# Seven products for eight in a quarter of the contraction: two output projections and one gate of a decoder trunk

## The chip, the cores and the metric

The kernel runs on one core of a Trainium2 chip. The metric is device time in microseconds of one execution of the whole program. TensorE (PE) multiplies, VectorE (DVE) and ScalarE (ACT) do the work on elements, GpSimd (POOL) and SyncE (SP) mostly issue DMAs. Each engine takes its instructions in the order in which they were built.

## What is computed

The reference is a decoder trunk of two layers on 256 tokens of 2048 features, in float32. Each layer has a norm, a wide input projection, a token mixer (two recurrences in layer 0, a matrix memory in layer 1), an output projection added to the residual `h`, and a gated embedding. The lines that matter here, for both layers `i`:

```python
h = x
for i in range(DEPTH):
    ...
    mix = y @ e_w_out[j]            # layer 0; layer 1: yc @ o_w_out[j]
    h = h + mix
    pl = rmsnorm(p[i] @ ple_w[i], ple_norm[i])
    h = h + jax.nn.sigmoid(h @ ple_gate_w[i]) * pl
return rmsnorm(h, final_norm)
```

All the products of `h` or `y` with a 2048 x 2048 matrix are alike: 256 tokens, 2048 inputs, 2048 outputs.

## The kernel before

**A product.** Each float32 operand is split into a high and a low part, and three matmuls (high by high, high by low, low by high) stand for one. The activations are stationary: `act[j]` (tiles `ahl`) holds 256 input features of all 256 tokens, high and low. The weights move. A product with a 2048 x 2048 matrix goes in four chunks of 512 outputs; a chunk has two token halves of 128, each with its own PSUM bank, and takes the 2048 inputs in four quarters (`quarter_tok`, line 185). A quarter of one token half is 4 x 3 = 12 matmuls of 512 columns, so a chunk is 96. A quarter's weights come as two pieces of 128x1024 (512 KB each), read by SP into a ring of five tiles (`raw`). ACT casts each piece to its high part (`whi`, line 135) and DVE subtracts that to get the low part (`wlo`, line 136), in rings of four.

**Order of the work.** The program is written as generators. `project_two` (line 171) interleaves the quarters of chunks 0 and 1, so that a product can begin when only the first input features are there; `chunks` (line 180) appends the chunks 2 and 3. Side work (hops, splits of new activations, norms) is put into lanes and taken a step at a time by `pump` after each first token half. A scheduler then orders each engine's instructions by priority: loads' splits stand 400 ahead of their place in the text, other work at its place. `tc.issue_after(ins)` ties what is traced under it behind `ins` on the same engine.

**Seven for eight.** The first layer-1 gates (`oog`, `oz`) already use a scheme in which two chunks of outputs, two token halves and two halves of a quarter (or of two quarters) form a 2 x 2 by 2 x 2 block product: seven products of combinations of blocks stand for eight products of blocks. `combos` (line 231) makes four combinations of the activations (numbers 1 to 4, tiles `q4`) and splits them; `seven` (line 262) loads four weight pieces X, Y, W, Z of the quarter, adds them into each other on DVE, splits each state, and issues seven products of six matmuls into four PSUM banks A, F, E, B. The quarters that are left out of the scheme go through `plain` (line 222). After the first product (A) ACT copies A's bank to F and, negated, to B; E begins with the product of combination 4 and the state of Y. Halves are combined from PSUM and from SBUF tiles named `pr`.

**After a chunk.** In an output projection (`out_proj`, line 553) DVE adds both banks to the residual tile `hq[c]`. In the gate (`ple_gate`, line 565) ACT takes a tanh and two fused DVE operations scale it and add it to `hq[c]`. Then `to_features` (line 519) turns the chunk into the next product's activations: DVE transposes blocks (tile `w`, line 523), POOL writes them to DRAM and reads them back in four gathers (`across`, line 639 and 642), and ACT and DVE split them. The gathers wait in POOL's queue for the write to land.

**The residual tiles** `hq` are four tiles of 128 x 1024. In layer 0 POOL reads them from the input `x` (`load_hq`, line 1064): two before the output projection, the other two from within `mixed` (line 1070), at the chunks 1 and 2, each tied behind the last hop issued. In layer 1 POOL reads all four from DRAM copies (`home`, line 1382) before the output projection.

## Time and profile before

| | us |
|---|---|
| time, median of 3 runs | 1027.11 (1026.71 to 1027.2) |
| time of the profiled execution | 1026.88 |
| its span, first to last instruction | 1025.1 |
| TensorE busy | 1015.3 |
| DVE busy | 787.6 |
| ACT busy | 632.2 |
| POOL busy | 105.2 |

The profile is of one execution. Times of rows count from the first instruction. Matmuls overlap, so that a row's own length (0.39) is longer than the step from one to the next. L and a number is a line of the kernel before; a tile is named without its number.

### The profile page before, as it was taken

The numbers are of one execution on the slowest core, as the hardware profiler recorded it, in microseconds if no ns is written. First come the engines' busy times: TensorE is split into PE (matmuls) and PEld (weight loads), VectorE is DVE, ScalarE is ACT, GpSimd is POOL, SyncE is SP. The second block draws the span as 40 slices with busy tenths as digits, with TensorE's granted clock in tenths as the row PEclk, the third lists the DMA queues.
The fourth block names the chain that finished last, engine by engine and source line by source line (L and its number), as shares of the span: only waits on it lengthen the run. The fifth ranks groups of instructions, "written<-read, shape, count | busy, mean of one in ns | idle before, by whom it ended". The sixth has DMA issues, their size and how long they took to land. (4 is left out here: it accounts for less than half of the span.)

```text
span 1025.1 us, 14447 instructions
## 1 busy us (share of the span) xinstructions
PE 1015.3 (99%) x5188; PEld 843.8 (82%) x5188; DVE 787.6 (77%) x1163; ACT 632.2 (62%) x909; POOL 105.2 (10%) x190
## 2 busy tenths in 40 slices
PE   9999999999999999999999999999999999999996
PEld 8888888888888888888888888888888888888886
DVE  7858968969685775776559997878889996766684
ACT  7775554686974344565457876766676777344562
POOL 0111101011112121021011100000011112111000
PEclk9999999999999999999999999999999999999999
DMA  9988756568788898698798755357879889788652
GB/s 356 340 223 252 221 177 199 170 201 240 221 262 285 271 283 256 222 307 255 224 297 246 231 184 190 124 188 200 257 193 285 222 279 337 248 254 260 222 185 82
DMA packets 69672, 242.14 MB, mean 236 GB/s; under 512 B 9024, under 2 KB 10432, under 8 KB 69600
## 3 DMA queue, kind: packets, MB, share of 16 engines
q1 hardware_dynamic: 54720, 193.36, 57.4%
q0 software_dynamic: 14448, 47.33, 17.2%
q8 instruction: 40, 0.66, 0.3%
q10 hardware_dynamic: 432, 0.52, 0.1%
q14 instruction: 32, 0.26, 0.1%
HBM read 221.26 MB, written 19.92 MB: 235 GB/s over the span
## 5 line engine op out<-in xcount | busy, mean ns | idle before, releaser
L136 DVE TENSOR_TENSOR wlo<-raw,whi 128x1024 fp32r<-128x1024 f32 (+1 forms) x329 | 396.8, 1215 | 164.7 <-ACT whi L135 155.4
L135 ACT CAST whi<-raw 128x1024 fp32r<-128x1024 f32 (+1 forms) x329 | 343.6, 1048 | 258.2 <-PE mm L198 184.0
L196 PE MATMUL mm<-whi,ahl 128*128 128x512 f32 x960 | 375.1, 391 | 0.0
L197 PE MATMUL mm<-wlo,ahl 128*128 128x512 f32 x960 | 373.7, 389 | 0.0
L198 PE MATMUL mm<-whi,ahl 128*128 128x512 f32 x960 | 373.6, 389 | 0.0
L196 PEld LDWEIGHTS mm<-whi,ahl 128*128 128x128 f32 x960 | 180.2, 188 | 38.0 <-issue 0.8
L198 PEld LDWEIGHTS mm<-whi,ahl 128*128 128x128 f32 x960 | 180.2, 188 | 37.5
L197 PEld LDWEIGHTS mm<-wlo,ahl 128*128 128x128 f32 x960 | 180.3, 188 | 37.0
L217 PE MATMUL mm<-whi,ahl 128*128 128x512 f32 x244 | 77.9, 390 | 0.8 <-ACT mm L314 0.8
L196 PE MATMUL mx<-whi,ahl 128*128 128x512 f32 x160 | 62.2, 389 | 0.0
L197 PE MATMUL mx<-wlo,ahl 128*128 128x512 f32 x160 | 62.2, 389 | 0.0
L198 PE MATMUL mx<-whi,ahl 128*128 128x512 f32 x160 | 62.2, 389 | 0.0
L207 DVE TENSOR_TENSOR wlo<-ch,whi 128x1024 fp32r<-128x1024 f32 x41 | 49.5, 1222 | 8.2 <-ACT whi L206 6.9
L217 PEld LDWEIGHTS mm<-whi,ahl 128*128 128x128 f32 x244 | 45.8, 188 | 10.6 <-ACT mm L314 1.3
L217 PE MATMUL mm<-wlo,ahl 128*128 128x512 f32 x122 | 47.5, 390 | 0.0
L206 ACT CAST whi<-ch 128x1024 fp32r<-128x1024 f32 x41 | 42.8, 1053 | 7.6 <-PE mm L217 5.4
L217 PE MATMUL mx<-whi,ahl 128*128 128x512 f32 x128 | 41.6, 389 | 0.0
L217 PE MATMUL mm<-whi,q 128*128 128x512 f32 x112 | 37.1, 389 | 0.0
L197 PEld LDWEIGHTS mx<-wlo,ahl 128*128 128x128 f32 x160 | 30.0, 188 | 6.3
L196 PEld LDWEIGHTS mx<-whi,ahl 128*128 128x128 f32 x160 | 30.0, 188 | 6.2
L198 PEld LDWEIGHTS mx<-whi,ahl 128*128 128x128 f32 x160 | 30.0, 188 | 6.2
L217 PEld LDWEIGHTS mx<-whi,ahl 128*128 128x128 f32 x128 | 24.0, 188 | 5.0
(372 smaller groups left out, 1129.1 us busy)
## 6 DMA issues: line engine op xcount, KB each, us to landing
raw<-in_ew_dram SPq DMA_DIRECT2D x64, 512.0 KB, 5.0
raw<-in_g_dram SPq DMA_DIRECT2D x64, 512.0 KB, 4.6
raw<-in_eo_dram SPq DMA_DIRECT2D x32, 512.0 KB, 5.6
raw<-in_oqk_dram SPq DMA_DIRECT2D x32, 512.0 KB, 4.4
raw<-in_ov_dram SPq DMA_DIRECT2D x32, 512.0 KB, 4.2
raw<-in_oo_dram SPq DMA_DIRECT2D x32, 512.0 KB, 5.3
raw<-in_oog_dram SPq DMA_DIRECT2D x24, 512.0 KB, 4.1
raw<-in_oz_dram SPq DMA_DIRECT2D x20, 512.0 KB, 5.2
```

The source lines that it names most:

```text
L135: last["act"] = s.copy(h, r).ins
L136: last["dve"] = v.tensor_tensor(out=l, in0=r, in1=h.bitcast(F32), op=ALU.subtract).ins
L196: te.matmul(ps[hf], xh, wh, start=(k == 0), stop=False)
L197: te.matmul(ps[hf], xh, wl, start=False, stop=False)
L198: last["pe"] = te.matmul(ps[hf], xl, wh, start=False, stop=(k == KT - 1)).ins
L206: last["act"] = s.copy(hi, r).ins
L207: last["dve"] = v.tensor_tensor(out=lo, in0=r, in1=hi.bitcast(F32), op=ALU.subtract).ins
L217: last["pe"] = te.matmul(o, x, y, start=(first and k + i == 0), stop=(end and k == n - 1 and i == 2), skip_group_check=True).ins
```

## The change

It does four things.

1. A new generator `two_and_seven` takes the place of `chunks` in both output projections and in the first gate (`g0`). Chunks 0 and 1 stay as they are; chunks 2 and 3 go through `seven`, with the scheme on the first quarter of the contraction (512 inputs) and the three other quarters plain. The combinations are started when chunk 0 has been handed on, and drained when chunk 1 has.
2. In the two output projections `seven` is given `home`, the first token half of `hq[3]`: ACT copies it into bank E after the copies of A, E's product accumulates onto it, and the last sum goes straight into `hq[3]`, so that the add for that half falls away. Without `home` (the gate, and the older uses) E begins with its product. In layer 0, `hq[2]` and `hq[3]` are now read at chunk 0 and chunk 1.
3. In `product`, the first matmul is tied behind the last matmul traced before it, so that the products of a section stand on TensorE in the order of the text.
4. `combos` works on a whole pair of token halves at once: combinations 3 and 1 in one tile and one split, then 2 and 4 in another.

The core of the diff:

```diff
+    def two_and_seven(w, act, before, places, home=None):
+        qs = {}
+        for c, ps in enumerate(project_two(w, act, before)):
+            for hf in range(2):
+                yield c, hf, ps[hf]
+            if c == 0:
+                room, part, *where = places()
+                start("combos", combos(act, 0, qs, *where))
+        drain("combos")
+        for b, hf, src in seven(w, 2, act, qs, (0,), room, part, home and home()):
+            yield 2 + b, hf, src
...
-                last["pe"] = te.matmul(o, x, y, start=(first and k + i == 0), stop=(end and k == n - 1 and i == 2),
-                                       skip_group_check=True).ins
+                with ExitStack() as behind:
+                    if k + i == 0:
+                        behind.enter_context(tc.issue_after(last["pe"]))
+                    last["pe"] = te.matmul(o, x, y, start=(first and k + i == 0), stop=(end and k == n - 1 and i == 2),
+                                           skip_group_check=True).ins
...
+        a11, a21 = whole(0)
+        a12, a22 = whole(1)
+        c, (c3, c1) = pair()
+        less(c3, a21, a11)
+        less(c1, a21, a22)
+        keep(c, (3, 1))
         yield
+        d, (c2, c4) = pair()
+        less(c2, a11, c1)
+        less(c4, a12, c2)
+        keep(d, (2, 4))
         yield
...
         with tc.high_priority(offset=450):
             s.copy(F, A)
             s.activation(B, A, AF.Copy, scale=-1.0)
+            if home is not None:
+                s.copy(E, home)
         Y = load(room, 1, 1)
-        product(E, combo(4), split(Y), True)
+        product(E, combo(4), split(Y), home is None)
...
-        soon(g, E, g, ALU.add)
-        yield 1, 0, g
+        if home is None:
+            soon(g, E, g, ALU.add)
+            yield 1, 0, g
+        else:
+            soon(home, E, g, ALU.add)
+            yield 1, 0, None
...
-        for c, ps in enumerate(chunks(a["eo"], 4, y, ready(y, "fm"))):
-            if c in (1, 2):
-                load_hq(c + 1, last["hop"])
+        for c, hf, src in two_and_seven(a["eo"], y, ready(y, "fm"), in_e0, lambda: hq[3][:, 0]):
+            if hf == 0 and c < 2:
+                load_hq(c + 2, last["hop"])
...
-    acth = ple_gate(hq, a["g0"], act, pls, rp0, hss0, "on", "fg", ready(act, "fe"), gate_sums)
+    acth = ple_gate(hq, two_and_seven(a["g0"], act, ready(act, "fe"), in_e0), pls, rp0, hss0, "on", "fg", gate_sums)
...
-        act = out_proj(hq, chunks(a["oo"], 4, y, ready(y, "fm")), "fo")
+        act = out_proj(hq, two_and_seven(a["oo"], y, ready(y, "fm"), in_m1, lambda: hq[3][:, 0]), "fo")
```

How instructions stand now, in layer 0's output projection. TensorE first, before: the end of chunk 1 (bank `mx_3064`) and the beginning of chunk 2 (bank `mm_3407`).

```order
L196 MATMUL mx_3064<-whi_3364,ahl_3286 128x512
L197 MATMUL mx_3064<-wlo_3365,ahl_3286 128x512
L198 MATMUL mx_3064<-whi_3364,ahl_3286 128x512
L196 MATMUL mm_3407<-whi_3410,ahl_2785 128x512 [waits Activation_49]
L197 MATMUL mm_3407<-wlo_3411,ahl_2785 128x512 [waits DVE_49]
L198 MATMUL mm_3407<-whi_3410,ahl_2785 128x512
L196 MATMUL mm_3407<-whi_3410,ahl_2785 128x512
```

And now: `mx_3426` is bank A, `mm_3428` is bank E, `q4_3423` holds combinations 2 and 4, `whi_3447` and `wlo_3448` are the split of Y.

```order
L211 MATMUL mx_3064<-whi_3367,ahl_3286 128x512
L233 MATMUL mx_3426<-whi_3432,ahl_2785 128x512 [waits Activation_49]
L233 MATMUL mx_3426<-wlo_3433,ahl_2785 128x512 [waits DVE_49]
L233 MATMUL mx_3426<-whi_3432,ahl_2785 128x512 x2
L233 MATMUL mx_3426<-wlo_3433,ahl_2785 128x512
L233 MATMUL mx_3426<-whi_3432,ahl_2785 128x512
L233 MATMUL mm_3428<-whi_3447,q4_3423 128x512 [waits DMAHW3_49,DMAHW2_49,DMAHW6_49,DVE_49,Activation_49]
L233 MATMUL mm_3428<-wlo_3448,q4_3423 128x512 [waits DVE_49]
L233 MATMUL mm_3428<-whi_3447,q4_3423 128x512 [waits DVE_49]
L233 MATMUL mm_3428<-whi_3447,q4_3423 128x512
L233 MATMUL mm_3428<-wlo_3448,q4_3423 128x512
```

Chunk 2 began with a quarter that needs only activations and weights; now it begins with A, and E, which needs a combination, stands directly behind A.

DVE at the same place, before: from the first add of chunk 1 (`hq_3059<-mx_3063`) on.

```order
L560 TENSOR_TENSOR hq_3059<-mx_3063,hq_3059 128x512
L515 TENSOR_TENSOR pl_153<-pl_153,row_3341 128x512
L136 TENSOR_TENSOR wlo_3448<-raw_3446,whi_3447 128x1024
L560 TENSOR_TENSOR hq_3059<-mx_3064,hq_3059 128x512
L136 TENSOR_TENSOR wlo_3454<-raw_3452,whi_3453 128x1024
L523 STREAM_TRANSPOSE w_3397<-hq_3059 128x4x4x32 x2
L515 TENSOR_TENSOR pl_157<-pl_157,row_3341 128x512
```

And now: `ch_3430`, `ch_3445`, `raw_3457` are X, Y, W; `wlo_3463` and `wlo_3469` belong to the plain quarter behind E, `wlo_3499` to the product behind that; `w_3349` is the transpose of chunk 0, `w_3410` that of chunk 1, and `q4_3423` the low part of combinations 2 and 4.

```order
L549 STREAM_TRANSPOSE w_3349<-hq_3057 128x4x4x32
L304 TENSOR_TENSOR raw_3457<-raw_3457,ch_3430 128x1024
L136 TENSOR_TENSOR wlo_3463<-raw_3461,whi_3462 128x1024
L136 TENSOR_TENSOR wlo_3469<-raw_3467,whi_3468 128x1024
L304 TENSOR_TENSOR ch_3430<-ch_3430,ch_3445 128x1024
L220 TENSOR_TENSOR wlo_3499<-raw_3457,whi_3498 128x1024
L586 TENSOR_TENSOR hq_3059<-mx_3064,hq_3059 128x512
L264 TENSOR_TENSOR q4_3391<-qc_3388,q4_3391 128x512
L549 STREAM_TRANSPOSE w_3410<-hq_3059 128x4x4x32 x2
L255 TENSOR_TENSOR qc_3420<-xr_3384,qc_3388 128x256
L541 TENSOR_TENSOR pl_153<-pl_153,row_3343 128x512
L255 TENSOR_TENSOR qc_3420<-xr_3386,qc_3420 128x256
```

The low part `q4_3423` is the row behind these. The sums of the weights and three splits that TensorE uses after E now stand between chunk 0's transpose and the combinations that E uses. In the first gate and in layer 1's output projection the same six weight operations stand ahead of combinations 2 and 4.

POOL's queue, before: `hq_3393` is `hq[2]`, `hq_3557` is `hq[3]`.

```order
L639 DMA dfe0_3351<-w_3347 128x1024
L642 DMA r_3350<-dfe0_3351 32x4x256 x4
L1064 DMA hq_3393<-in_x_dram 128x2x512
L639 DMA dfe1_3401<-w_3397 128x1024
L642 DMA r_3400<-dfe1_3401 32x4x256 x4
L1064 DMA hq_3557<-in_x_dram 128x2x512
L639 DMA dfe2_3565<-w_3561 128x1024
```

And now: `hq_3337` is `hq[2]`, `hq_3406` is `hq[3]`.

```order
L1092 DMA hq_3337<-in_x_dram 128x2x512
L533 DMA row_3343<-in_rows_dram 128x1024
L533 DMA row_3345<-in_rows_dram 128x1024
L1124 MEMSET wg_3789 128x512
L667 DMA dfe0_3353<-w_3349 128x1024
L670 DMA r_3352<-dfe0_3353 32x4x256 x4
L1092 DMA hq_3406<-in_x_dram 128x2x512
L667 DMA dfe1_3414<-w_3410 128x1024
```

`hq[2]` moved ahead of the first hop, and `hq[3]` from behind the second hop to behind the first.

## The prediction

> **What bounds the kernel now.** I read the page first, then the waits of TensorE, the stretches around the three places that change, and the timelines of VectorE (DVE), GpSimd (POOL) and ScalarE (ACT) there.

> ```profile
> span 1025.1 us, 14447 instructions
> PE 1015.3 (99%) x5188; PEld 843.8 (82%) x5188; DVE 787.6 (77%) x1163; ACT 632.2 (62%) x909; POOL 105.2 (10%) x190
> PE mm L217 <- ACT mm L314: 0.8, 1, 0.8
> PE st L97 <- PEq L1634: 0.8, 1, 0.8
> 686.95 21.76 PE mm L217 x96
> ```

> TensorE works through 1015.3 of 1025.1 us, and its table of waits holds only 1.6 us. So the time is the number of matmuls times their rate, and the rate stands in the last row (the chain of waits): 96 matmuls of 512 columns begin within 21.76 us, 0.2267 us each. Anything else costs time only if it makes TensorE wait; a wait of TensorE, on the other hand, costs its full length, since there is no slack to take it up.

> The second halves (chunks 2 and 3) of the three products, in the table by stretches (columns: PE, PEld, DVE, ACT, POOL busy, clock, DMA share, GB/s), and the first matmul of chunk 2 in each, from PE's timeline:

> ```profile
> 344.10:387.60 43.50, 43.50 (x193) 36.02 (x192) 32.18 (x42) 19.22 (x25) 9.18 (x16) 1.00 0.93 288
> 431.00:475.00 44.00, 44.00 (x206) 35.75 (x205) 29.52 (x34) 25.90 (x40) 9.09 (x17) 1.00 0.95 295
> 886.60:930.10 43.50, 43.50 (x194) 36.03 (x193) 27.68 (x34) 19.31 (x25) 7.70 (x14) 1.00 0.85 267
> ...
> 343.45 0.39 PE L196 MATMUL mm<-whi,ahl 128*128 128x512 f32 x1
> ...
> 430.49 0.39 PE L196 MATMUL mm<-whi,ahl 128*128 128x512 f32 x1
> ...
> 885.58 0.39 PE L196 MATMUL mm<-whi,ahl 128*128 128x512 f32 x1
> ```

> TensorE is busy throughout, DVE for 28 to 32 us of each. I call the moment at which chunk 1's last matmul is issued T: 343.45 (output projection of layer 0), 430.49 (first gate), 885.58 (output projection of layer 1). A quarter of one chunk on one token half is 12 matmuls, 2.72 us, so chunk 0's two banks are ready at about T - 8.16 and T - 5.44 (plus a matmul's own 0.39), chunk 1's at T - 2.72 and T.

> **The change part by part.** *Fewer matmuls.* Each of the three sections has seven products of six matmuls for eight: 18 matmuls less, 18 x 0.2267 = 4.08 us off TensorE. This is all that the change can gain; nothing in the trace speaks against it.

> *More work on DVE and ACT.* Each section casts and splits seven weight pieces where it had four, adds pieces four times, builds four combinations of the activations, and combines halves through SBUF. The prices are start-to-start in DVE's timeline (a row's own length overlaps the next by about 0.08):

> ```profile
> 339.08 0.68 DVE L560 TENSOR_TENSOR hq<-mm,hq 128x512 f32<-128x512 f32 x1
> 339.68 1.21 DVE L136 TENSOR_TENSOR wlo<-raw,whi 128x1024 fp32r<-128x1024 f32 x1
> 340.81 0.70 DVE L523 STREAM_TRANSPOSE w<-hq 128x512 f32<-128x512 f32 x1
> 341.44 0.65 DVE L560 TENSOR_TENSOR hq<-mx,hq 128x512 f32<-128x512 f32 x1
> ...
> 644.43 0.42 DVE L255 TENSOR_TENSOR xr<-xr 128x256 f32<-128x256 f32 x1
> 644.76 0.42 DVE L236 TENSOR_TENSOR xr<-ahl 128x256 f32<-128x256 f32 x1
> ...
> L284 DVE TENSOR_TENSOR ch<-ch,raw 128x1024 f32<-128x1024 f32 x8 | 9.5, 1220 | 0.1
> ...
> L135 ACT CAST whi<-raw 128x512 fp32r<-128x512 f32 x4 | 2.5, 622 | 0.9 <-DMA raw<-in_pw_dram 0.8
> ...
> L314 ACT COPY mm<-mx 128x512 f32<-128x512 f32 x4 | 2.3, 579 | 0.2
> ```

> So 0.60 us for 128x512, 0.63 for a transpose, 1.13 for a split or an add of 128x1024 (both last 1.22), 0.33 for 128x256. Per section: 3 splits (3.4), 4 adds (4.5), the combinations (4 x 0.60 + 4 x 0.33 = 3.7), three more half-chunk operations (1.8): 13.4 us more on DVE. In bulk this would fit: 32.2 + 13.4 = 45.6 against 42.2 of TensorE in the worst section, of which 3.7 can run before T. The question is what stands ahead of what.

> *The products in program order.* TensorE now issues A (six matmuls), then E (six), then the plain quarters. E is due 1.36 us after T. It multiplies Y by combination 4, which shares a tile and a split with 2 and is the last that `combos` makes, and TensorE, waiting for them, can issue nothing behind: the splits that it would free, and so the weight loads, wait too. DVE reaches those combinations late, since the built order puts six weight operations of the products that follow E ahead of them.

> Layer 0's output projection: the adds of chunk 0 can start at T - 7.8. In the new order follow, up to the second transpose of chunk 0: add 0.60, sum of a high and a low part 0.60, transpose 0.63, two differences 0.66, split 1.13, add 0.60, split 1.13, add 0.60, weight add 1.13, transpose 0.63, in sum 7.7: T - 0.1. Then to the last difference: weight add 1.13, two splits 2.26, weight add 1.13, split 1.13, add 0.60, low part of the first pair 0.60, two transposes 1.26, difference 0.33, gain row 0.60, difference 0.33, in sum 9.4: T + 9.3. The cast on ACT (0.62) gives T + 9.9: DVE alone makes E wait some 8.6 us, and 0.4 more for the low part, which E's third matmul needs.

> *The residual inside E.* In both output projections E starts from a copy of hq[3]. In layer 0 that tile is read from DRAM by POOL's queue, and the change brings it forward to the place that hq[2] had, behind the hop of chunk 0 (write to DRAM, four gathers that wait for it to land). POOL's timeline and the page's list of DMA issues:

> ```profile
> 341.82 0.54 POOL L639 DMA_DIRECT2D dfe<-w  x1 [14.22 <-DVE w L523]
> 346.82 2.22 POOL L642 DMA_DIRECT2D r<-dfe  x4 [4.46 <-DMA dfe<-w]
> 349.03 0.72 POOL L1064 DMA_DIRECT2D hq<-in_x_dram  x1
> ...
> hq<-in_x_dram POOLq DMA_DIRECT2D x4, 512.0 KB, 8.8
> ```

> The hop begins when the second transpose of chunk 0 ends: in the trace at 340.81 + 0.70 = 341.5, T - 1.9; in the new order at T - 0.1, 1.8 later. So the tile is issued at 349.03 + 1.8 = 350.8 (T + 7.4), lands 8.8 later (T + 16.2) and is copied on ACT in 0.58: T + 16.8. That is later than the combinations, and it is E's wait: 16.8 - 1.36 = **15.4 us**. Behind the copy on ACT stand the casts of the next weights; they are not what TensorE needs first. In layer 1 the four tiles have POOL's queue to themselves before chunk 0's hop, so I take no wait from there.

> Layer 1's output projection has the same order on DVE, without the gain row and with four tiny operations of 0.1 to 0.2 us before the last difference: T + 9.2, cast T + 9.8, low part 0.4: **8.9 us**.

> The first gate has no residual in E, but tanh and two fused operations a half stand on DVE instead of one add:

> ```profile
> 422.53 0.60 ACT L572 ACTIVATE th<-mm 128x512 f32<-128x512 f32 x1 [1.66 <-PE mm L198]
> ...
> 423.16 0.69 DVE L573 SCALAR_TENSOR_TENSOR th<-th,pl 128x512 f32<-128x512 f32 x1 [1.04 <-ACT th L572]
> 423.89 0.76 DVE L574 SCALAR_TENSOR_TENSOR hq<-th,rp,hq 128x512 f32<-128x512 f32 x1
> 424.68 0.71 DVE L523 STREAM_TRANSPOSE w<-hq 128x512 f32<-128x512 f32 x1
> ...
> 427.69 0.68 DVE L573 SCALAR_TENSOR_TENSOR th<-th,pl 128x512 f32<-128x512 f32 x1
> 428.41 0.75 DVE L574 SCALAR_TENSOR_TENSOR hq<-th,rp,hq 128x512 f32<-128x512 f32 x1
> 429.07 0.68 DVE L573 SCALAR_TENSOR_TENSOR th<-th,pl 128x512 f32<-128x512 f32 x1
> ```

> Its first fused operation starts at 423.16, T - 7.33, and a pair takes 0.73 + 0.66 (one that does not wait for itself). From there stand four pairs (about 5.6 with the short waits), eight weight operations (9.0), four transposes (2.5), four differences (1.3), one low part (0.6): 19.0, T + 11.7. Cast 0.62 and semaphores 0.1: T + 12.4; less 1.36, and 0.4 for the low part: **11.5 us**.

> *The four older sections of seven products* keep their order but for one matmul, which stood ahead of E and waited 0.8 us for ACT's copy of A. E now stands there, and DVE's splits are close behind: I take 0, between -0.8 and +0.5.

> *The clock.* None of the old waits is long; the only long pause of TensorE is the one behind its last matmul:

> ```profile
> 1013.50:1016.90 3.40, 3.40 (x29) 3.24 (x28) 1.51 (x6) 0.51 (x2) 0.00 (x0) 1.00 0.69 257
> 1016.90:1020.30 3.40, 0.04 (x1) 0.00 (x0) 2.61 (x10) 2.81 (x5) 0.00 (x0) 1.00 0.00 0
> 1020.30:1025.10 4.80, 0.00 (x0) 0.00 (x0) 0.73 (x2) 0.56 (x2) 0.00 (x0) 0.50 0.59 219
> ...
> 0.78 3.75 PE L97 MATMUL st<-const-float32-1.0 128*128 128x128 f32 x16 [0.78 <-PEq L1634]
> ...
> 4.18 1.20 PE L476 MATMUL mx<-whi,ahl 128*128 128x256 f32 x4
> ...
> L476 PE MATMUL mx<-whi,ahl 128*128 128x256 f32 x8 | 2.1, 445 | 0.0
> ...
> L1469 PE MATMUL mm<-whi,ahl 128*128 128x256 f32 x16 | 4.5, 282 | 0.0
> ```

> The granted clock falls to 0.50 some 3.4 us after the last matmul, and my three pauses are all longer. How long it stays down once work resumes, only the start can tell: its eight first 256-column matmuls last 445 ns where later ones last 282; they begin at 4.18 and take 2.1 us, so that they are over at about 6.3, 5.5 us after the first matmul at 0.78. At half rate that is at most 2.75 us lost per pause; the least is 0. I take 2.5, close to the start's, since the matmuls behind each pause are dense: 7.5 us for three.

> [...]

> Sum, against the profiled execution's 1026.88 us (its span of 1025.1 and 1.8 around it; the three timed runs have their median at 1027.11): 1026.9 - 4.1 + 15.4 + 11.5 + 8.9 + 7.5 = **1066.1**.

> **The rivals.** *Faster.* If E never waits, only the 4.1 us count: 1022.8. That needs combinations 2 and 4, and hq[3], within 1.4 us after T in all three sections, or work that TensorE does meanwhile. Against it: six weight operations of 1.13 us ahead on DVE, and an issue at T + 5.6 even in the old trace. [...]

> *The clock holds or recovers at once.* Same pauses, no slow matmuls behind them: 1066.1 - 7.5 = 1058.6. For it: no pause inside the old trace shows the loss.

> *hq[3] comes earlier than I work out* (a shorter hop, a landing in the shadow of idle weight queues). Then DVE decides in layer 0 as well, at 9.0 instead of 15.4: 1059.7.

> *DVE stays behind after E.* If the 13.4 us more per section are not caught up during the pause, TensorE waits again at the later products, up to 45.6 - 42.2 = 3.4 us in the worst section, perhaps 6 in all: 1072.

> **How the numbers follow.** The forecast (three pauses and a clock that falls) has 0.70, the clock that holds 0.11, the earlier hq[3] 0.08, DVE behind 0.07, faster 0.04. The first four lie above the old time by 3% or more. The range goes from 1054, below the two cheaper cases by the error of my chains (about 10% of 36 us), to 1076, above the dearest by the same. A measurement of this kernel can tell about 0.2% (2 us) from no change: faster 0.04, within it 0.01, slower 0.95.

> **What would show it.** In the changed kernel's waits of TensorE, three waits of the new product line for ACT or DVE, of about 15, 11.5 and 9 us, at E right behind A in each section; 18 records of TensorE fewer, apart from those that a trace misses; a granted clock of 0.50 in stretches of 5 us behind each; hq[3] landing some 16 us after T in layer 0. It is wrong if those waits are short, if they stand elsewhere, or if the clock stays at 1.00.

## The result, and the profile after

| | before | after |
|---|---|---|
| median of the runs, us | 1026.9 (1026.71 to 1027.2) | 1065.17 (1064.0 to 1066.12) |
| ratio, 95% interval | | 1.0371 [1.0358, 1.0384] |
| profiled execution, us | 1026.88 | 1064.8 |

The change makes the kernel 3.7% slower. The page after:

```profile
span 1063.0 us, 14489 instructions
PE 1017.3 (96%) x5170; PEld 843.4 (79%) x5170; DVE 825.1 (78%) x1207; ACT 650.9 (61%) x934; POOL 105.2 (10%) x190
```

TensorE's waits (line, who was waited for, us in all, times, longest):

```profile
PE mm L233 <- ACT q L263: 19.4, 2, 11.2
PE mm L233 <- ACT mm L337: 15.2, 1, 15.2
PE mm L233 <- DVE vl L1351: 0.9, 1, 0.9
```

The 18 records are gone (5188 to 5170), and TensorE, which waited 1.6 us in all, now waits 34.6 in three places. PE's timeline shows where, with A's last matmul ahead of each, and A's first in layer 0:

```profile
343.55 0.39 PE L233 MATMUL mx<-whi,ahl 128*128 128x512 f32 x1
...
344.68 0.39 PE L233 MATMUL mx<-whi,ahl 128*128 128x512 f32 x1
360.30 0.80 PE L233 MATMUL mm<-whi,q 128*128 128x512 f32 x1 [15.23 <-ACT mm L337]
...
447.77 0.39 PE L233 MATMUL mx<-whi,ahl 128*128 128x512 f32 x1
459.41 0.79 PE L233 MATMUL mm<-whi,q 128*128 128x512 f32 x1 [11.25 <-ACT q L263]
...
462.95 0.40 PE L233 MATMUL mx<-whi,ahl 128*128 128x512 f32 x1
...
914.66 0.39 PE L233 MATMUL mx<-whi,ahl 128*128 128x512 f32 x1
923.20 0.79 PE L233 MATMUL mm<-whi,q 128*128 128x512 f32 x1 [8.15 <-ACT q L263]
```

The prediction's T is read here at that first row, 343.55: it names T after chunk 1's last matmul, but the rows that it shows for it, and its figures, are of chunk 2's first, one step of 0.23 us later.

Each wait stands at E, right behind A. From A's last start to E's first it takes 15.62, 11.64 and 8.54 us, where one step is 0.2267: 15.39 + 11.41 + 8.31 = 35.1 us lost. Two timelines say who was late. In layer 0 it is the tile hq[3], read by POOL and copied by ACT (L337), although VectorE's last combination (L255) was ready 7 us before:

```profile
343.81 0.54 POOL L667 DMA_DIRECT2D dfe<-w  x1 [16.09 <-DVE w L549]
347.00 2.22 POOL L670 DMA_DIRECT2D r<-dfe  x4 [2.65 <-DMA dfe<-w]
349.20 0.71 POOL L1092 DMA_DIRECT2D hq<-in_x_dram  x1
...
352.40 0.42 DVE L255 TENSOR_TENSOR qc<-xr,qc 128x256 f32<-128x256 f32 x1
...
352.85 0.62 ACT L263 CAST q<-qc 128x512 fp32r<-128x512 f32 x1 [5.73 <-DVE qc L255]
359.65 0.59 ACT L337 COPY mm<-hq 128x512 f32<-128x512 f32 x1 [6.18 <-DMA hq<-in_x_dram]
```

In the other two sections the cast of combinations 2 and 4 (L263) waits for VectorE, and E begins as it ends:

```profile
457.87 0.84 DVE L255 TENSOR_TENSOR qc<-xr,qc 128x256 f32<-128x256 f32 x2
...
458.74 0.62 ACT L263 CAST q<-qc 128x512 fp32r<-128x512 f32 x1 [1.20 <-DVE qc L255]
...
922.07 0.42 DVE L255 TENSOR_TENSOR qc<-xr,qc 128x256 f32<-128x256 f32 x1
...
922.53 0.62 ACT L263 CAST q<-qc 128x512 fp32r<-128x512 f32 x1 [4.91 <-DVE qc L255]
```

Behind each E the first eight steps are slow: in the gate the ninth matmul begins at 462.95, 3.54 us after the first, where eight steps of 0.2267 make 1.81, so 1.7 us are lost; in layer 0 1.8, in layer 1 1.9, in sum 5.4. The account: 35.1 + 5.4 - 4.08 = 36.4 of the 37.9 us between the two profiled executions. The other 1.5 are steps a little over 0.2267 us (0.7) and a longer stretch behind the last matmul (0.8; last section).

### The profile page after: what moved, and what is told of

Same layout as the page of the kernel before. It is cut to its first block, busy times and chain, and to the rows that moved or that the text cites. A ratio compares the mean times of both kernels' runs of the same rounds, so it can differ in the third digit from the quotient of the medians.

```text
span 1063.0 us, 14489 instructions
## 1 busy us (share of the span) xinstructions
PE 1017.3 (96%) x5170; PEld 843.4 (79%) x5170; DVE 825.1 (78%) x1207; ACT 650.9 (61%) x934; POOL 105.2 (10%) x190
## 4 chain that ended last, share of the span: by engine, by line
PE 90%; DVE 3%; issue 3%; DMA 2%; ACT 1%; POOL 0%; ACTq 0%; DVEq 0%; POOLq 0%
PE mm L233 21%; PE mm L209 16%; PE mm L210 16%; PE mm L211 16%; PE mx L233 7%; PE mx L210 3%; PE mx L211 3%; PE mx L209 3%; PE mm L502 1%; DMA hq<-in_x_dram 1%; PE mx L502 1%; PE mm L1507 1%; PE mm L1508 1%; PE mm L1506 1%; PE nu L1316 1%
## 5 line engine op out<-in xcount | busy, mean ns | idle before, releaser
L136 DVE TENSOR_TENSOR wlo<-raw,whi 128x1024 fp32r<-128x1024 f32 (+1 forms) x317 | 382.1, 1214 | 163.9 <-ACT whi L135 155.1
L135 ACT CAST whi<-raw 128x1024 fp32r<-128x1024 f32 (+1 forms) x317 | 331.3, 1048 | 248.4 <-PE mm L211 118.5
L209 PE MATMUL mm<-whi,ahl 128*128 128x512 f32 x768 | 300.3, 391 | 0.0
L210 PE MATMUL mm<-wlo,ahl 128*128 128x512 f32 x768 | 299.1, 389 | 0.0
L211 PE MATMUL mm<-whi,ahl 128*128 128x512 f32 x768 | 298.9, 389 | 0.0
L209 PEld LDWEIGHTS mm<-whi,ahl 128*128 128x128 f32 x768 | 144.2, 188 | 30.4 <-issue 0.4
L211 PEld LDWEIGHTS mm<-whi,ahl 128*128 128x128 f32 x768 | 144.2, 188 | 30.1
L233 PE MATMUL mm<-whi,ahl 128*128 128x512 f32 x472 | 150.2, 390 | 0.0
L233 PEld LDWEIGHTS mm<-whi,ahl 128*128 128x128 f32 x472 | 88.6, 188 | 18.8 <-issue 0.4
L233 PE MATMUL mm<-wlo,ahl 128*128 128x512 f32 x236 | 91.9, 389 | 0.0
L233 PE MATMUL mm<-whi,q 128*128 128x512 f32 x160 | 57.4, 412 | 35.5 <-ACT q L263 19.4
L220 DVE TENSOR_TENSOR wlo<-ch,whi 128x1024 fp32r<-128x1024 f32 x56 | 67.5, 1221 | 10.2 <-ACT whi L219 8.4
L233 PE MATMUL mx<-whi,ahl 128*128 128x512 f32 x224 | 74.0, 394 | 0.0
L219 ACT CAST whi<-ch 128x1024 fp32r<-128x1024 f32 x56 | 58.2, 1053 | 14.5 <-PE mm L211 6.8
L233 PEld LDWEIGHTS mm<-whi,q 128*128 128x128 f32 x160 | 31.5, 197 | 44.1 <-ACT q L263 20.2
L209 PE MATMUL mx<-whi,ahl 128*128 128x512 f32 x160 | 62.2, 389 | 0.0
L210 PE MATMUL mx<-wlo,ahl 128*128 128x512 f32 x160 | 62.2, 389 | 0.0
L211 PE MATMUL mx<-whi,ahl 128*128 128x512 f32 x160 | 62.2, 389 | 0.0
L233 PEld LDWEIGHTS mx<-whi,ahl 128*128 128x128 f32 x224 | 43.1, 192 | 9.4
L233 PE MATMUL mx<-wlo,ahl 128*128 128x512 f32 x112 | 44.3, 395 | 0.0
## 6 DMA issues: line engine op xcount, KB each, us to landing
raw<-in_ew_dram SPq DMA_DIRECT2D x64, 512.0 KB, 4.8
raw<-in_g_dram SPq DMA_DIRECT2D x62, 512.0 KB, 4.5
raw<-in_oqk_dram SPq DMA_DIRECT2D x32, 512.0 KB, 4.9
raw<-in_ov_dram SPq DMA_DIRECT2D x32, 512.0 KB, 4.2
raw<-in_eo_dram SPq DMA_DIRECT2D x30, 512.0 KB, 4.6
raw<-in_oo_dram SPq DMA_DIRECT2D x30, 512.0 KB, 4.7
raw<-in_oog_dram SPq DMA_DIRECT2D x24, 512.0 KB, 4.3
raw<-in_oz_dram SPq DMA_DIRECT2D x20, 512.0 KB, 5.0
```

Source lines behind the costliest of these rows:

```text
L135: last["act"] = s.copy(h, r).ins
L136: last["dve"] = v.tensor_tensor(out=l, in0=r, in1=h.bitcast(F32), op=ALU.subtract).ins
L209: te.matmul(ps[hf], xh, wh, start=(k == 0), stop=False)
L210: te.matmul(ps[hf], xh, wl, start=False, stop=False)
L211: last["pe"] = te.matmul(ps[hf], xl, wh, start=False, stop=(k == KT - 1)).ins
L219: last["act"] = s.copy(hi, r).ins
```

## The experiments

**Theory.** E stands directly behind A by program order, while its inputs come 8 to 15 us later; that, and the clock that falls meanwhile, is the cost. **Rivals.** The extra work of VectorE is the cost by itself, wherever E stands; or the slow steps and the wait in layer 0 have other causes. Unless it says otherwise, each kernel is the changed one with the edit shown. Where a run has one time only, the text compares waits, since one time can be off by 2 us and more (last section).

### Without the program order

```
-                    if k + i == 0:
-                        behind.enter_context(tc.issue_after(last["pe"]))
```

> The changed kernel without its third part: the first matmul of a product need not be issued behind the matmul before it in the program, so the scheduler may put other products or plain quarters ahead of E; every added operation on VectorE and ScalarE stays. My theory (the pauses stand at E only because TensorE is made to meet E first, while its inputs come 8 to 15 us later; the work of the section fits beside TensorE in bulk): the three waits of 15.2, 11.2 and 8.3 us shrink to some 0 to 3 us each, no stretch of granted clock 0.50 is left before the end, and the time is 1023 to 1030 us, within 0.4% of the kernel before on either side. The rival (the added 13.4 us of VectorE work per section are themselves the cost, so that TensorE waits for them wherever E stands): waits of 8 us or more a section at other products, time 1050 us or more.

Measured: 1030.59 us, ratio 1.0035 [1.002, 1.0049]. Its waits of TensorE:

```profile
PE mm L231 <- ACT mm L332: 3.4, 4, 1.2
PE mm L231 <- ACT whi L135: 0.9, 1, 0.9
```

The scheduler puts plain quarters behind A, nothing long is left, and the granted clock stays at 1.00 until the last matmul (its mean over the execution is 0.997, as against 0.983 in the changed kernel). So 34.6 of the 38.3 us go with the order, and the first rival falls. The time is 0.6 us above the range that I gave, and it is not the 1022.8 of fewer matmuls either: the plain quarter behind A waits for ACT's copy of A (L332) in its stead, 3.4 us in all with the older section's 0.8.

### The residual tile early

```
-            if hf == 0 and c < 2:
-                load_hq(c + 2, last["hop"])
             if (c, hf) == (0, 0):
+                for n in (2, 3):
+                    load_hq(n, last["hop"])
```

> The changed kernel, with hq[3] read from DRAM at chunk 0 beside hq[2], ahead of the hop of chunk 0 on GpSimd's queue, in layer 0. My theory (in layer 0 E waits for the copy of hq[3], whose DMA stands behind the hop; VectorE's combinations come next): only the wait in layer 0 changes, from 15.2 to about 9 us, the waits of 11.2 and 8.3 in the other two sections stay; 1064.8 - 6 = about 1058.5 us. The rival (the combinations are as late as the tile, or the pause comes from the transfer's contention with the weights): the wait stays above 13 us, and the time within 2 us of 1064.8.

PE's timeline (A's first and last matmul, E's first):

```profile
345.59 0.39 PE L233 MATMUL mx<-whi,ahl 128*128 128x512 f32 x1
...
346.73 0.39 PE L233 MATMUL mx<-whi,ahl 128*128 128x512 f32 x1
355.56 0.79 PE L233 MATMUL mm<-whi,q 128*128 128x512 f32 x1 [8.45 <-ACT q L263]
```

And the waits:

```profile
PE mm L233 <- ACT q L263: 27.8, 3, 11.2
```

All three waits are now for the cast of combinations; the one in layer 0 is 8.45 us instead of 15.23, the others are as they were. That is what the theory says. The time, 1062.1 us (one run), is 3.6 above what I expected: A begins at 345.59, where the changed kernel has it at 343.55, so 2.0 us were lost before anything that the edit touches, and the slow steps behind the three pauses cost some 2 us more (2.9, 2.3 and 2.2; last section).

### E one place later

```
-        product(E, combo(4), split(Y), home is None)
+        y0 = split(Y)
+        if not j == 2 or two:
+            product(E, combo(4), y0, home is None)
...
         plain(w, j, rest[0], act, (A, F))
+        if j == 2 and not two:
+            product(E, combo(4), y0, home is None)
```

(In the three sections only; the others keep their order.)

> The changed kernel, with E's product written one place later in the three sections: behind the first plain quarter, 24 matmuls of 0.227 us or 5.4 us. My theory (the wait ends at a moment that VectorE, ScalarE and the DMA set, not TensorE): each wait is shorter by what TensorE does meanwhile, 15.2 to about 10, 11.2 to about 6, 8.3 to about 3, some of it given back if the plain quarter's own inputs are late (up to 2 us each); 1064.8 - 16.3 = 1048.5 us, up to 1054 with what is given back. The rival (E's inputs are late because TensorE stands, since the buffers that the splits need come free only with its matmuls): E's inputs come earlier by the same 5.4 us, no wait or next to none is left in the section of layer 1, and the time is under 1043 us.

Measured: 1051.24 us (one run). The waits of TensorE in the three sections:

```profile
PE mm L233 <- ACT q L263: 10.0, 2, 6.1
PE mm L233 <- ACT mm L337: 6.5, 1, 6.5
PE mx L233 <- ACT mm L335: 4.0, 3, 1.7
```

E waits 6.5, 6.1 and 3.9 us instead of 15.2, 11.2 and 8.1, and the plain quarter ahead of it waits 1.7 at most for the copies of A. The time is 13.6 us below the profiled execution of the changed kernel, within the range of the theory. The wait in layer 0 shrank by more than 5.4: the tile, issued at the same time, had landed 1.9 us sooner.

### TensorE busy through the pause

```
+    fillers = [60, 45, 30]
...
+        if j == 2 and not two:
+            idle = pst.tile([P, 512], F32, name="st", tag="st")
+            for _ in range(fillers.pop(0)):
+                with tc.issue_after(last["pe"]):
+                    last["pe"] = te.matmul(idle[:, 0:P], fill, fill, start=True, stop=True).ins
         Y = load(room, 1, 1)
```

> The changed kernel, with 60, 45 and 30 matmuls of ones (128x128, written to a tile that nobody reads, 0.21 us each, so 12.8, 9.6 and 6.4 us) between A and E in the three sections, which keep TensorE at work during most of each pause without any use. My theory (the granted clock falls to 0.50 because TensorE stands for more than some 3 us, and costs matmuls at half rate behind E): E begins when it did before, the granted clock stays at 1.00 in the three stretches, the eight or nine slow matmuls behind each E are gone, and the time is 1064.8 - 5.4 = about 1059.4 us. The rival (the slow steps behind E come from weight loads or inputs that are late, not from the clock): the steps stay at 0.4 us and the time at 1063 to 1067 us.

Measured: 1059.2 us (one run), 5.6 less with 135 useless matmuls more (the trace has two records for each, and 30.6 us of TensorE's time for all, 0.23 each); 0.6 of it is a quicker start, ahead of any edit. The stretches behind the three E (PE, PEld, DVE, ACT, POOL, clock):

```profile
357.50:363.50 6.00, 4.79 (x23) 3.84 (x22) 1.23 (x1) 1.64 (x2) 2.19 (x4) 1.00 0.37 116
455.00:461.00 6.00, 4.80 (x21) 3.53 (x21) 2.71 (x5) 1.66 (x2) 3.31 (x6) 1.00 0.47 130
917.00:923.00 6.00, 4.46 (x21) 3.28 (x21) 4.53 (x20) 1.67 (x2) 0.56 (x1) 1.00 0.97 251
```

The clock stays at 1.00 and the slow steps are gone: in the gate the ninth matmul from E's first on begins 2.22 us after it (456.53 to 458.75) instead of 3.54. So they came from the clock, and the clock from the pause.

### Combinations first, tile late

```
-                start("combos", combos(act, 0, qs, *where))
-        drain("combos")
+                with tc.high_priority(offset=900):
+                    for _ in combos(act, 0, qs, *where):
+                        pass
```

> The changed kernel, with the combinations put first on VectorE at chunk 0 in all three sections; hq[3] of layer 0 still read behind the hop. My theory (in layer 0 the tile alone makes a wait of some 15 us, in the other two the combinations do): in layer 0 the wait stays at 13 to 16 us, in layer 1 it falls from 8.3 to the 1.8 us of the copy on ScalarE, in the gate, where the combinations then stand ahead of the fused operations, from 11.4 to between 2 and 8: 1064.8 - (0 to 2) - 6.5 - (3 to 9) - (1.7 to 3.4 of slow clock) = 1044 to 1054 us. The rival (the combinations decide in layer 0 as well): there a wait under 5 us, and a time under 1043 us.

Measured: 1048.1 us (one run). POOL's and ACT's timeline at the tile of layer 0:

```profile
347.03 0.72 POOL L1093 DMA_DIRECT2D hq<-in_x_dram  x1
...
354.50 0.59 ACT L338 COPY mm<-hq 128x512 f32<-128x512 f32 x1 [7.70 <-DMA hq<-in_x_dram]
```

And the waits:

```profile
PE mm L234 <- ACT mm L338: 12.1, 2, 10.4
PE mm L234 <- ACT q L264: 7.1, 1, 7.1
```

The gate and layer 1 do as expected (7.1 and, as 12.1 - 10.4, 1.7 us), and in layer 0 the tile still decides, with a wait of 10.4 us. I had 13 to 16: with the combinations out of the way VectorE gets to chunk 0's transpose sooner, so the tile is issued 2.2 us earlier (347.03 for 349.20; 0.3 of it because A itself begins at 343.22 for 343.55), and it takes about 7.4 us to land instead of 10.4.

### Everything made first, the order kept

```
+        if at_once:
+            before(0)
+            room, part, *where = places()
+            start("combos", combos(act, 0, qs, *where))
...
+                with tc.high_priority(offset=900):
+                    for _ in combos(act, 0, qs, *where):
+                        pass
...
+        if home is not None:
+            s.copy(E, home)
         X = load(room, 0, 0)
         product(A, quadrant(0, 0), split(X), True)
...
-            if home is not None:
-                s.copy(E, home)
```

`at_once` holds for the first gate and layer 1; layer 0 has the lines with the offset, at chunk 0. hq[3] is read early, as above.

> The changed kernel with its seven products and its program order, but with what E needs made first: hq[3] of layer 0 read at chunk 0, the combinations begun at the start of the section in the first gate and in layer 1 and put first at chunk 0 in layer 0, and the copy of hq[3] into E's bank written ahead of A, so that it doesn't stand behind A's two copies on ScalarE. My theory (late inputs were the whole cost of the program order): no wait at E over 0.5 us in the three sections, no stretch of clock 0.50, and what is left is the 18 matmuls less: 1026.9 - 4.1 = 1022.8, up to 1.5 us given back elsewhere, so 1022.8 to 1024.5 us, a ratio of 0.996 to 0.998. The rival (VectorE's added work only moves, and the splits that it delays stop TensorE at other places): waits of 1 to 5 us elsewhere, 1026 us or more.

Measured: 1027.25 us, ratio 0.9996 [0.9987, 1.0005]: the 38 us are gone with the program order in place, no wait at E is left in the three sections, and the clock stays at 1.00 until the end (its mean is 0.997). But it is no faster than before, where I had expected 1022.8 to 1024.5. Its waits that the profiled execution before doesn't have:

```profile
PE mm L239 <- DVE wlo L136: 1.3, 2, 0.7
PE mx L508 <- ACT whi L477: 0.9, 1, 0.9
```

And the timeline of VectorE and TensorE ahead of the first of the two:

```profile
453.69 0.69 DVE L150 TENSOR_TENSOR ahl<-xr,ahl 128x512 fp32r<-128x512 f32 x1 [2.65 <-ACT ahl L149]
454.30 0.69 DVE L605 SCALAR_TENSOR_TENSOR th<-th,pl 128x512 f32<-128x512 f32 x1
455.02 0.75 DVE L606 SCALAR_TENSOR_TENSOR hq<-th,rp,hq 128x512 f32<-128x512 f32 x1
455.69 0.69 DVE L150 TENSOR_TENSOR ahl<-xr,ahl 128x512 fp32r<-128x512 f32 x1
456.29 1.22 DVE L136 TENSOR_TENSOR wlo<-raw,whi 128x1024 fp32r<-128x1024 f32 x1
...
457.57 0.50 PE L239 MATMUL mm<-wlo,ahl 128*128 128x512 f32 x1 [0.65 <-DVE wlo L136]
```

The low parts of two plain quarters come late; ahead of the first split, VectorE stands 2.65 us for the next stage's activations and then has four other operations. Here the rival was right, in its time (1026 us or more) and in kind: waits have moved elsewhere. Against the profiled execution before, PE's timeline loses 2.2 us more in the gate (0.8 at each of the two splits, the rest in short gaps), 0.8 in steps a little over 0.2267 us, 0.6 in the first 25 us, and 0.8 behind the last matmul: 4.4 us for the 4.1 saved.

### The copy of hq[3] behind A's two

The same kernel, with `s.copy(E, home)` left where the change has it.

> As the kernel with everything made first, except that the copy of hq[3] into E's bank stands where the change put it, behind A's two copies on ScalarE. In the run with hq[3] early, A's last matmul began at 346.73 and the three copies at 347.15, 347.63 and 348.12 (0.60 long), so E can begin at about 348.8, where it was due at 346.96. My theory: two waits of ScalarE of about 1.8 us at E, one in each output projection, none over 0.5 in the gate: 3.6 us more than the kernel with everything made first, about 1026.4 to 1028 us. The rival (other casts on ScalarE, not the two copies, hold the copy up): waits as short as without, 1022.8 to 1024.5 us, or far longer than 3 us.

The wait of TensorE:

```profile
PE mm L239 <- ACT mm L343: 3.3, 2, 1.7
```

Two waits of 1.66 us at E, one in each output projection, as expected; from start to start 2.05 instead of 0.23. The time, 1032.05 us (one run), is 4.8 above the kernel with everything made first instead of 3.6; in this run A's last matmul in layer 0 already came 1.6 us later (346.83 for 345.20).

### No order, inputs sooner

The first experiment, with hq[3] early and the combinations of the gate and of layer 1 begun at the start of their sections.

> The changed kernel without its program order, with hq[3] of layer 0 read at chunk 0 and the combinations of the first gate and of layer 1 begun at the start of their sections; the copy of hq[3] still behind A's two copies on ScalarE. My theory (free order hides late inputs, but the plain quarter that then follows A waits for A's copy): one wait of 0.8 us behind A in each output projection as in the first experiment, next to none in the gate (there 1.4 and 1.1 before): 1030.6 - 2.4 to 1030.6 - 4 = 1026.5 to 1028.5 us. The rival (free order itself loses what the first experiment lost, wherever the inputs stand): within 1 us of 1030.6.

Measured: 1029.04 us, ratio 1.002 [1.0011, 1.0029]; 1.5 us less than the first experiment, where I expected 2.4 to 4. The waits in the output projections are the expected 0.8 us each from start to start, but one as long, for a split, stays in the gate. Inconclusive between the two, and 1.8 us slower than the order with its inputs ready (which also has the copy of hq[3] ahead of A).

### One step of side work less

```
-            plain(w, j + 1, kq, act, (E, B), end=(kq == 3))
+            plain(w, j + 1, kq, act, (E, B), end=(kq == 3), pumps=(j != 2 or kq != 1))
```

> The kernel with everything made first, with one step less of the interleaved side work in each of the three sections: the plain quarter that follows the last product lets no side work in between its two halves, so that in the gate the next stage's activations (the split of ahl, for which VectorE stands 2.65 us until the hop has landed) come behind the next two splits of weights and not ahead of them. My theory (the two waits of 0.81 us at 456.5 and 458.9 stem from splits that stand behind that split of ahl in VectorE's order): both waits under 0.3 us, 1.3 us less, about 1025.5 to 1026 us. The rival (VectorE is simply short of time there, and another wait takes their place): within 0.5 us of the kernel with everything made first, or slower.

Measured: 1028.56 us, ratio 1.0015 [1.0006, 1.0024]: slower, and the rival was right. Its waits in the three sections:

```profile
PE mx L239 <- DVE wlo L136: 1.6, 1, 1.6
PE mm L239 <- DVE wlo L136: 1.5, 2, 0.9
```

Both waits of the gate stay, 0.85 the first of them, with VectorE still standing for the activations ahead of the split (the idle time is 2.89 us there), and a new one of 1.6 us appears in layer 0. My cure moved other steps than I meant; that VectorE's queue order causes the waits is neither shown nor excluded by it.

### Seven products in the output projections alone

The kernel with everything made first, and the gate with four plain chunks, as before the change.

> The kernel with everything made first, with the first gate as it was before the change (four plain chunks); only the two output projections have seven products. In the kernel with everything made first, the profiled run ended at 1027.25 us: 4.1 us less of matmuls against some 2.9 us of short waits in the gate (two of 0.81 us for late splits of plain quarters among them), 0.6 more at the start and 0.8 more behind the last matmul. My theory (those waits are what the added work in the gate costs, where VectorE has tanh's two fused operations a half besides): without it 2.9 us of waits go and 6 matmuls, 1.36 us, come back: 1.5 us less, about 1025.5 us, a ratio of 0.997 to 0.9995. The rival (the waits in the gate come from something that the change does not touch there, or move on to the next section): 1027 us or more.

Measured: 1024.97 us, ratio **0.9981 [0.9973, 0.999]**, the fastest of all: 0.2% below the kernel before, and the interval leaves out 1. Its waits of TensorE, whole (the profiled execution took 1026.62 us, more than nine of the other ten; it loses 5.9 us in its first 25):

```profile
PE mm L239 <- DVE vl L1357: 0.9, 1, 0.9
PE st L97 <- PEq L1679: 0.8, 1, 0.8
PE mx L508 <- ACT whi L477: 0.5, 1, 0.5
```

None is left in the sections that the change touches. Two output projections save 12 matmuls, 2.7 us, and 2.0 us are seen. With the gate's section, 6 matmuls fewer, the kernel was 2.3 us slower by the medians and 1.5 by the ratios (whose intervals just overlap): in the gate the scheme saves nothing, and probably costs more than it saves. VectorE's total time does not explain it: with everything made first, VectorE is busy for 41.4 of 42.2 us in the second half of layer 0's output projection (343.8 to 386.0), where TensorE never waits, and for 35.9 of 42.0 us in that of the gate (431.0 to 473.0), where it does.

### The order alone

The kernel before, with program order for the products that it had.

> The kernel before with the third part of the change alone: products in program order in the four sections that had seven products already, no new section. My theory (program order costs only where the inputs are late, and in these sections VectorE's splits are close behind): E then stands where the stray matmul stood that waited 0.8 us, with about the same wait, and the time is within 0.15% of the kernel before, 1025.5 to 1028.5 us. The rival (program order costs by itself, since it takes from TensorE the work that it could do meanwhile): waits of 2 us or more in each of the four sections, 1032 us or more.

Measured: 1027.03 us, ratio 1.0002 [0.9993, 1.0011], one wait of 0.9 us at E. The order costs nothing where the inputs are there.

## Why the prediction was right, and where it was off

- **The result.** 1066.1 us forecast, 1065.17 measured. The mechanism holds: three pauses at E, the order that makes them (34.6 us go without it), the inputs that are late (all go with them ready). That the number is so near is partly luck: the waits and the slow steps came to 35.1 + 5.4 = 40.5 us where the forecast has 43.3, and 1.5 us that it doesn't have (steps a little longer, a longer end) make up half of the difference.
- **Fewer matmuls, 4.08 us.** 18 records gone. But with every input ready the term shows in the time only in part: 2.0 of 2.7 us in the output projections, nothing in the gate. I had said that nothing in the trace speaks against it. Why the gate gives nothing stays open; that its fused operations leave VectorE no time is not shown, and VectorE's busy time there (35.9 of 42.0 us) speaks against it.
- **Layer 0, 15.4 us.** Measured 15.39. Two errors cancelled, by luck: with T at 343.55 the tile was issued at T + 5.7, not T + 7.4 (the hop's write landed 1.8 us sooner than in the old trace), and took 10.4 us to land instead of 8.8 (the median of four tiles in the old trace; the one issued there at 349.03 took 9.3), so that it landed at T + 16.1, for T + 16.2. The second input was at T + 9.9, as forecast, and with the tile early E waited 8.6 from start to start: the 9.0 of the rival.
- **Gate, 11.5 us.** 11.41 and a share of the slow low part. VectorE's last difference ended at 458.71 with T at 446.64: T + 12.1, forecast T + 11.7.
- **Layer 1, 8.9 us.** 8.31 and that share. Last difference at 922.49, T = 913.53: T + 9.0, forecast T + 9.2.
- **The clock, 7.5 us.** The term that was most off in this execution. I took 2.5 a pause from the start's 5.5 us until full clock, with 0.4 us for the low part beside it in the gate and in layer 1; the changed kernel shows 1.8, 1.7 and 1.9 with the low part in it, 5.4 in all, since the clock is back 3.5 to 3.9 us after E begins. The size is not fixed: with the tile early the clock was back only 4.6 to 6.0 us after E's start, and the three pauses cost 2.9, 2.3 and 2.2 us, 7.5 in all, with the low part in it.
- **The older sections, 0.** The wait there is 0.9 us, and the order alone makes no difference.
- **The rivals.** *Clock holds*: excluded by the steps behind E, which take 0.43 us and not 0.2267, and so is *behind after E*: the changed kernel's table has no other wait in the three sections. *Faster*, at 1022.8 if E never waits: its condition was met in the kernel with everything made first, and it took 1027.25. The price of that rival was wrong by 4 us: I had priced only the wait at E. Short waits in the gate (2.2 us, two late splits of 0.8 among them), longer steps, a slower start and a longer end take back what the matmuls save.

## What to carry to other kernels

A product that is pinned to program order has to find its inputs ready: list every input (combinations, residual, weights), follow each through the queue that it stands in (hq[3], which needs nothing of the hop, was issued at 349.20, behind the hop that began at 343.81), and move the latest ahead first. Saving matmuls at a bound TensorE paid in two sections here (taken together) and not in the third, and the busy share of the engine that does the extra work did not tell which; try the scheme section by section. Price the case "no wait there" with the wait that comes next.

## What the runs showed of the hardware

**The granted clock changed on a grid.** Stretches of 3.41 us of the changed kernel, on both sides of a change of the clock (the number ahead of the last two is the clock):

```profile
346.83:350.24 3.41, 0.00 (x0) 0.00 (x0) 3.41 (x5) 0.29 (x1) 2.92 (x5) 1.00 0.91 240
350.24:353.65 3.41, 0.00 (x0) 0.00 (x0) 2.73 (x7) 0.62 (x1) 0.59 (x1) 0.50 1.02 201
360.48:363.89 3.41, 3.41 (x9) 2.67 (x10) 0.00 (x0) 0.58 (x1) 2.19 (x4) 0.50 0.32 91
363.89:367.30 3.41, 3.41 (x16) 2.81 (x15) 1.23 (x1) 0.46 (x1) 0.00 (x0) 1.00 0.41 95
449.23:452.64 3.41, 0.00 (x0) 0.00 (x0) 3.41 (x4) 1.55 (x3) 0.00 (x0) 1.00 0.74 219
452.64:456.05 3.41, 0.00 (x0) 0.00 (x0) 3.28 (x7) 1.82 (x4) 0.56 (x1) 0.50 0.93 341
459.47:462.88 3.41, 3.41 (x8) 2.69 (x9) 0.61 (x1) 0.50 (x1) 3.12 (x6) 0.50 0.64 155
462.88:466.29 3.41, 3.41 (x16) 2.78 (x16) 1.23 (x1) 0.54 (x1) 0.57 (x2) 1.00 0.94 326
916.86:920.27 3.41, 0.00 (x0) 0.00 (x0) 3.41 (x5) 0.76 (x1) 2.22 (x4) 1.00 0.78 247
920.27:923.68 3.41, 0.48 (x1) 0.48 (x2) 3.31 (x16) 0.62 (x1) 0.56 (x1) 0.50 1.02 216
923.68:927.10 3.42, 3.42 (x9) 2.52 (x9) 1.33 (x8) 0.89 (x1) 0.00 (x0) 0.50 0.92 280
927.10:930.51 3.41, 3.41 (x16) 2.81 (x16) 1.23 (x1) 0.15 (x1) 1.90 (x4) 1.00 0.32 84
```

In the changed kernel the clock fell 5.2, 4.5 and 5.2 us behind the end of the last matmul ahead of the three pauses, of which the shortest is 8.3 us, and 2.8 us behind that of the last matmul of all. The two pauses of 1.8 us in the kernel with the copy behind A's two left it up: in both output projections the steps behind E's first matmul are at most 0.34 us, and 0.24 from the second on. Whether length alone decides is not shown: that execution has no wait of TensorE over 1.7 us, and its mean granted clock is 0.995, where the kernel with everything made first has 0.997.

**The start is not the same each time.** In the first 25 us, which no edit touches, the profiled runs lose between 3.3 and 6.2 us against steps at 0.2267 us for 512 columns. TensorE's wait there for ACT's cast of the weights (`whi`) is 0.2 us with the combinations first and 1.6 with the copy behind A's two. Two of the four that lose most (5.7 to 6.2) are the single times 1062.1 and 1032.05.

**A longer end.** From the end of the last matmul to that of the span it takes 8.8 to 9.2 us in the ten profiled kernels with seven products in the gate, and 8.2 in the three without. The slowest write of the output lands 3.7 us after its issue in the changed kernel, 2.8 in the one before. Why was not tried, and stays open.
